# Changing which transfers go first, and where one norm sum stands, in an eight-core decoder layer kernel

## The chip, the cores and the metric

The kernel runs on all 8 cores of one Trainium2 chip, one program per core, each core with its own share of the tokens. The metric is the device time of one launch in microseconds, which is that of the slowest core. Executions fall into a fast state and, now and then, a slow one in which the cores of one die, sometimes of both, run at a lower granted clock. Only fast runs are compared here, and the medians below leave slow runs out.

## The reference, cut to what matters

One decoder layer over 2080 tokens per core (2048 prompt tokens, 16 learned ones before them, 16 tokens of running sequences). Two mixers share one input projection, then comes a gated feed-forward part with a three-tap convolution over tokens. Each half has a norm before and a norm after it.

```python
def rmsnorm(x, g):
    xf = x.astype(jnp.float32)
    y = xf * lax.rsqrt(jnp.mean(xf * xf, axis=-1, keepdims=True) + EPS)
    return (y * g.astype(jnp.float32)).astype(x.dtype)
...
    h = rmsnorm(x, g_pre_mix)
    z = h @ w_in                                                      # (B,T,IN_TOTAL)
    u, v, bg, cg, ga, gb = jnp.split(z, IN_SPLITS, axis=-1)
    ...
    merged = jax.nn.sigmoid(ga) * a + jax.nn.sigmoid(gb) * b
    x = x + rmsnorm(merged @ w_o, g_post_mix)
    h = rmsnorm(x, g_pre_ffn)
    upc, new_ffn = causal_dwconv(h @ w_up, buf_ffn, w_ffn_conv)       # (B,T,2*D_FF)
    gate, val = jnp.split(upc, 2, axis=-1)
    y = (jax.nn.silu(gate) * val) @ w_down
    x = x + rmsnorm(y, g_post_ffn)
```

## The kernel before

Every operation is recorded first. A small scheduler, which models each engine in nanoseconds, then fixes the order of the instructions on each engine, before anything is compiled. Numbers in that model therefore do not change durations; they change orders. TensorE's main work keeps its recorded order. Norm sums are "floating" matmuls: they slip in when their input has been ready for `flt` nanoseconds of the model.

```python
                    if li < len(pe_flt) and not pe_flt[li].nd and (fi == len(pe_fix) or pe_flt[li].idx < pe_fix[fi].idx):
                        f = pe_flt[li]
                        sf = max(free[e], ready[f.idx])
                        if c is None or ready[f.idx] + (f.flt if f.pri > s + 8000.0 else 400.0) <= s or sf <= s - 200.0:
                            c, s = f, sf
# ... cut ...
    def rstd(sq, i, n, lo=0, flt=2500.0, sq2=None):
        tree(sq, n)                          # VectorE: 8 planes of squares to 2, two instructions
        sums([(sq, 0, 2)], n, lo, flt=flt)   # TensorE: sum over partitions, floating
        ln_exp(i, n, lo=lo, sq=sq2)          # ScalarE: reciprocal root
# ... cut ...
    def epi_n2(t):
        rstd(XSQ2[t], 0 if t == NTA - 1 else 2, TA[t], lo_of(t, LO), flt=2500.0 if t == NTA - 1 else 4000.0)
```

The front: x of tile 0 (512 tokens) comes in four quarters through SyncE's DMA queue. The weight blocks of `w_in` (524 KB each, cast to bf16 on the way) and then x of tile 1 (392 tokens, `X[1]`) come through GpSimd's queue. The first `M0` groups of tile 0 are multiplied before tile 1 begins. The first five work on x that is only scaled, and the norm is applied afterwards.

```python
    xs0 = [sp_dma(X[0].flat[:, 0:2 * N0], xT[0][:, 0:2 * N0], [], [X[0].t(0, 2)], 128 * 2 * N0 * 4,
                  pri=-1e6)]
# ... cut: constants, quarters 1 to 3 ...
    wd = [wload(W_IN, w_in, 0, 1, BL)]
    wd += [wload(W_IN, w_in, i, 1, BL, after=[xs0[0]]) for i in range(1, 16)]
# ... cut: other weights ...
    for q in range(4):
        pool_dma(X[1].flat[:, 2 * q * NA:2 * (q + 1) * NA], xT[1][:, 2 * q * NA:2 * (q + 1) * NA], [], [X[1].t(2 * q, 2)],
                 128 * 2 * NA * 4, after=[xs0[1]], pri=-1e6)

    warm(60)
# ... cut: squares and scaling of x0 ...
    for q in range(4):
        pe([(bank(SB, N0), ONES, XSQ2[0].ap[:, k, :]) for k in (2 * q, 2 * q + 1)], [ONESB.t(), XSQ2[0].t(2 * q, 2)],
           [("ps", SB)], N0, start=q == 0, stop=q == 3)
        if q < 3:
            warm(10)
    ln_exp(0, N0, sq=1)
# ... cut ...
    seq = [(0, i) for i in range(NRAW, M0)] + [(1, i) for i in range(NRAW)] + [(0, i) for i in range(M0, M1)]
```

`warm(n)` issues n dummy matmuls so that TensorE's clock is not halved while it waits.

Of the kernel before, what the change touches and what calls it, by code (L numbers as in the profile page):

```python
# [44 lines left out]
FSEQ = (("v", 0), ("c", 0), ("v", 1), ("c", 1), ("u", 0), ("b", 0), ("v", 2), ("c", 2),  # L45
        ("b", 1), ("v", 3), ("c", 3), ("b", 2), ("u", 1), ("b", 3), ("u", 2), ("u", 3))
NRAW = 5
M0, M1 = 6, 12
WIN_ORDER = [{"u": 0, "v": 4, "b": 8, "c": 12}[_k] + _c for _k, _c in FSEQ]
for _c in range(8):  # L50
    WIN_ORDER += [16 + _c, 24 + _c]
# [11 lines left out]
class Sched:  # L63
# [55 lines left out]
    def order(self):  # L119


        ops = self.ops
        for op in ops:
            op.succ = []
            op.nd = len(op.deps)
        for op in ops:
            for d in op.deps:
                ops[d].succ.append(op)
        at, t = {}, 0.0
        for op in ops:  # L130
            if op.eng == "pe" and not op.flt:
                at[op.idx] = t
                t += op.dur
        for op in reversed(ops):
            op.pri = at.get(op.idx, t + 1e5)
            for x in op.succ:
                op.pri = min(op.pri, x.pri - 100.0)
            if op.idx not in at:
                op.pri -= op.byts / 300.0 + 3000.0 if op.dma else 1.5 * op.dur
        ready = {}  # L140
        avail = {e: [] for e in self.ENGS}
        pe_fix = [op for op in ops if op.eng == "pe" and not op.flt]
        pe_flt = [op for op in ops if op.eng == "pe" and op.flt]
        fi = li = 0
        free = {e: 0.0 for e in self.ENGS}
        dma_free = {"sp": 0.0, "pool": 0.0}
        seqs = {e: [] for e in self.ENGS}
        ends = {"sp": [0.0] * 14, "pool": [0.0] * 16}
        tab = None
        cold = 0.0  # L150
        for op in ops:
            ready[op.idx] = 0.0
            if op.nd == 0:
                avail[op.eng].append(op)
        left = len(ops)
        while left:
            best = None
            for e in self.ENGS:
                a = avail[e]
                if e == "pe":  # L160
                    c = s = None
                    if fi < len(pe_fix) and not pe_fix[fi].nd:
                        c = pe_fix[fi]
                        s = max(free[e], ready[c.idx])
                    if li < len(pe_flt) and not pe_flt[li].nd and (fi == len(pe_fix) or pe_flt[li].idx < pe_fix[fi].idx):
                        f = pe_flt[li]
                        sf = max(free[e], ready[f.idx])
                        if c is None or ready[f.idx] + (f.flt if f.pri > s + 8000.0 else 400.0) <= s or sf <= s - 200.0:
                            c, s = f, sf
                    if c is None:  # L170
                        continue
                else:
                    if not a:
                        continue
                    s = max(free[e], min(ready[x.idx] for x in a))
                    c = min((x for x in a if ready[x.idx] <= s), key=lambda x: x.pri + x.off + (SWITCH if x.tab not in (None, tab) else 0.0) - (DMAEARLY if x.dma and e == "pool" else 0.0))
                    if c.tab not in (None, tab):
                        near = [x for x in a if x.tab == tab and ready[x.idx] <= s + 400.0]
                        if near:
                            c = min(near, key=lambda x: x.pri + x.off)  # L180
                            s = max(s, ready[c.idx])
                if best is None or s < best[0]:
                    best = (s, e, c)
            s, e, op = best
            avail[e].remove(op)
            if e == "pe":
                if op.flt:
                    li += 1
                else:
                    fi += 1  # L190
            left -= 1
            seqs[e].append(op)
            op.start = s
            if op.dma:
                s = max(s, ends[e].pop(0))
                free[e] = s + (650.0 if e == "pool" else 400.0)
                b, n = max(free[e], dma_free[e]), op.byts / 300.0
                if e == "sp" and dma_free["pool"] > b:
                    dma_free["pool"] += n
                    n *= 2.0  # L200
                dma_free[e] = b + n
                op.end = dma_free[e] + (3200.0 if e == "pool" else 2400.0)
                ends[e].append(op.end)
            elif e == "pe":
                if s - free[e] > 3400.0:
                    cold = s + 3500.0
                d = op.dur * (2.0 if s < cold else 1.0)
                free[e] = s + d
                op.end = free[e] + 165.0
            else:  # L210
                if op.tab not in (None, tab):
                    tab = op.tab
                    s += 1300.0
                op.end = s + op.dur
                free[e] = op.end + (30.0 if e == "pool" else -85.0)
            for x in op.succ:
                if x.eng == "pe":
                    lat = 0.0 if e == "pe" else 145.0
                elif op.dma:
                    lat = 600.0  # L220
                else:
                    lat = 180.0 if x.eng == "pool" else 100.0
                ready[x.idx] = max(ready[x.idx], op.end + lat)
                x.nd -= 1
                if x.nd == 0:
                    avail[x.eng].append(x)
        self.seqs = seqs
        self.model_end = max(op.end for op in ops)
# [51 lines left out]
def build_nc():  # L280
# [105 lines left out]
    H2S = [XSQ2[0]] + per_tile(KC, True, [o_h2s] * NTA)[1:4] + [XSQ2[4]]  # L386
    MERGED = per_tile(KC, True, [o_merged] * NTA)
    RAW = [MERGED[0], Buf(o_gt, KC, NA, True)]
    PS = [(0, 1), (2, 1)] + [(0, None)] * 3
    H = per_tile(KC, True, [o_h1 if t % 2 else o_h0 for t in range(NTA)])  # L390
    GT = per_tile(4, False, [o_gt] * NTA)
    POOLED = per_tile(4, True, [POOLB.off, o_h2s] + [POOLB.off] * 3)
# [61 lines left out]
    def act(fn, r, w, n, psum=False, ap=0, **k):  # L454
        S.add("act", fn, r, w, dur=n / 1.2 + (170 if psum else 200) + 93 * ap, **k)
# [65 lines left out]
    def ln_exp(i, n, sq=None, lo=0, ps_out=False):  # L521
        s = SD.ap[:, i, lo:n]
        out, tok = (bank(SB, n, lo), ("ps", SB)) if ps_out else (s, SD.t(i, 1))
        act(lambda e: e.activation(out=s, in_=bank(SB, n, lo), func=AF.Ln, bias=cc(C_EPS)),
            [("ps", SB), "eps"], [SD.t(i, 1)], n, psum=True, ap=1, tab="ln")
        if sq is not None:
            s2 = SD.ap[:, sq, lo:n]
            act(lambda e: e.activation(out=s2, in_=s, func=AF.Exp, scale=-1.0), [SD.t(i, 1)], [SD.t(sq, 1)], n, tab="ln")
        act(lambda e: e.activation(out=out, in_=s, func=AF.Exp, scale=-0.5), [SD.t(i, 1)], [tok], n, tab="ln")  # L529

    def rstd(sq, i, n, lo=0, flt=2500.0, sq2=None):
        tree(sq, n)
        sums([(sq, 0, 2)], n, lo, flt=flt)
        ln_exp(i, n, lo=lo, sq=sq2)
# [7 lines left out]
    def prenorm(t):  # L542
        for q in range(4):
            prenorm_sq(t, q)
        rstd(H[t], PS[t][0], TA[t], sq2=PS[t][1] if t == 1 else None)
        for k in range(KC):
            prenorm_h(t, k)

# [6 lines left out]
    def lo_of(t, lo):  # L555
        return lo if t == 0 else 0
# [190 lines left out]
                hook()  # L747

    def epi_n1(t):
        rstd(XSQ2[t], 0 if t == NTA - 1 else 1, TA[t], lo_of(t, LO), flt=5000.0 if t == NTA - 1 else 2500.0)  # L750

    def epi_r(t, q):
        N, lo = TA[t], lo_of(t, LO)
# [18 lines left out]
                   [R[t].t(4 * h, 4)], [("y", t, h)], 128 * 4 * N * 4)  # L772

    def epi_n2(t):
        rstd(XSQ2[t], 0 if t == NTA - 1 else 2, TA[t], lo_of(t, LO), flt=2500.0 if t == NTA - 1 else 4000.0)

    def epi_x(t, k):
        N, lo = TA[t], lo_of(t, LO)
# [119 lines left out]
    def warm(n):  # L898
        pe([(bank(6, 128), ONES, ONES)] * n, [ONESB.t()], [("ps", 6)], 128)
# [10 lines left out]
    S.add("pool", lambda e: e.memset(U.ap[:, :, 0:16], 0.0), [], [U.t()], dur=150)  # L910
    S.add("dve", lambda e: e.memset(cc(C_EPS), EPS), [KCST], ["eps"], dur=100)
    wd = [wload(W_IN, w_in, 0, 1, BL)]
    wd += [wload(W_IN, w_in, i, 1, BL, after=[xs0[0]]) for i in range(1, 16)]
    wload(W_POOL, w_pool, 0, 8, 128, after=[xs0[1]])
    for m in range(8):
        wd += [wload(W_IN, w_in, 16 + 2 * m + i, 1, BL, after=[xs0[1]]) for i in range(2)]
# [1 line left out]

    for q in range(4):
        pool_dma(X[1].flat[:, 2 * q * NA:2 * (q + 1) * NA], xT[1][:, 2 * q * NA:2 * (q + 1) * NA], [], [X[1].t(2 * q, 2)],  # L920
                 128 * 2 * NA * 4, after=[xs0[1]], pri=-1e6)

    warm(60)
    for q in range(4):
# [4 lines left out]
    for q in range(4):  # L929
        pe([(bank(SB, N0), ONES, XSQ2[0].ap[:, k, :]) for k in (2 * q, 2 * q + 1)], [ONESB.t(), XSQ2[0].t(2 * q, 2)],  # L930
           [("ps", SB)], N0, start=q == 0, stop=q == 3)
        if q < 3:
            warm(10)
    ln_exp(0, N0, sq=1)
    for i in range(NRAW):
        F_block(0, i)
# [65 lines left out]
    load_h2(0)  # L1002

    WD = {5: 0, 7: 1, 10: 2, 12: 3, 14: 4, 16: 5, 19: 6, 21: 7}
    WD1 = {7: 0, 9: 1, 11: 2, 13: 3, 15: 4, 17: 5, 19: 6, 21: 7}
    dn = [0]

    def wdn():
# [171 lines left out]
```

## Time and profile before

Median 826.31 us of 3 runs (824.86 to 827.02). All eight cores do nearly the same, so the table gives medians over the cores of the profiled run, with the range where it matters. "Half-clock loss" is half of the time in which TensorE was busy at a granted clock of 0.5.

| Profile before | us |
|---|---|
| x0's quarters land | 5.8, 9.9, 13.4, 16.1 |
| last part of X1 lands | 28.1 (27.5 to 29.1) |
| tile 1's first matmul, after 6 groups of tile 0 | 30.5 (29.2 to 31.1) |
| TensorE idle from 20 to 60 us; half-clock loss there | 0.80; 0.28 |
| TensorE idle from 340 to 440 us; half-clock loss there | 3.58; 1.67 |
| end of the core | 824.3 (818.5 to 825.8) |

TensorE is the full engine, so only its idle or half-clock time can be won, and it lies in two places: the front, and one gap near 400 us where TensorE stands still for a norm sum. The prediction below shows the lines.

To read them: PE, PEld, DVE, ACT, POOL and SP are TensorE, its weight loads, VectorE, ScalarE, GpSimd and SyncE. A timeline row gives start and duration in us, engine, line of the kernel, operation, what is written and read, shapes, count, and in brackets the idle time before it with what ended that. L469 is the helper through which all matmuls go, so its rows are told apart by their column counts (512 or 500 for tile 0, 392 for tile 1). A "tap" is one of VectorE's multiply-adds of the three-tap convolution; it reads a PSUM bank (TensorE's output buffer), which TensorE can write again only afterwards.

### The profile page before, as it was taken

Reading aid. Unit: us, or ns where it says so; the run is one execution under the profiler, and the core shown is the slowest. Engines: PE = TensorE matmul, PEld = TensorE weight load, DVE = VectorE, ACT = ScalarE, POOL = GpSimd, SP = SyncE. Lnnn points to the kernel's source line nnn. Section 1 sums busy time; section 2 is a strip of 40 time slices with the busy share of each in tenths; the row PEclk is TensorE's granted clock in tenths of the full one; section 3 lists DMA queues with packets and bytes.
Section 4 is the critical chain, followed back from the end, with each engine's and each line's share of the span. In section 5 each row is a group of like instructions: output and inputs, shape, how many; then the busy total and the mean of one; then the engine's idle time right before and its main releaser. Section 6 shows DMA issues by size and latency. Waiting matters only on the chain.

```text
span 825.8 us, 16706 instructions; the slowest of 8 cores (818.5 to 825.8 us)
## 1 busy us (share of the span) xinstructions
PE 801.0 (97%) x5108; PEld 499.0 (60%) x5108; DVE 564.7 (68%) x1054; ACT 452.1 (55%) x902; POOL 261.9 (32%) x297
## 2 busy tenths in 40 slices
PE   6999999999999999999899999999999999999994
PEld 4455455555555555566566666666666666666662
DVE  2997448786976686488985676568566765785723
ACT  3523284665565545586754565457456554665532
POOL 6432002001201262399532243225222522252231
PEclk8999999999999999999999999999999999999997
DMA  9999705766027899999970033014101500050063
GB/s 182 198 152 158 149 4 122 179 161 155 25 55 157 128 125 201 189 156 164 190 121 0 2 69 61 1 36 67 39 1 36 70 2 1 2 69 2 1 134 74
DMA packets 62838, 75.16 MB, mean 91 GB/s; under 512 B 3072, under 2 KB 59264, under 8 KB 62736
## 3 DMA queue, kind: packets, MB, share of 16 engines
q0 software_dynamic: 41440, 44.97, 38.2%
q1 hardware_dynamic: 21312, 29.14, 12.6%
q8 instruction: 43, 0.70, 0.3%
q14 instruction: 43, 0.35, 0.1%
HBM read 81.53 MB, written 22.90 MB: 126 GB/s over the span
## 4 chain that ended last, share of the span: by engine, by line
PE 92%; DMA 4%; DVE 2%; issue 1%; ACT 1%; DVEq 0%; SPq 0%; ACTq 0%; POOLq 0%
PE ps L469 92%; DMA big<-w_up 2%; DMA big<-xT 2%; DVE big L551 0%; DVEq L1051 0%; DVE big L820 0%; DVE big L864 0%; SPq L476 0%; DVE big L718 0%; ACT big L539 0%; ACT big L816 0%; DVE big L945 0%; ACT big L847 0%; DVE big L782 0%; DVE big L716 0%
## 5 line engine op out<-in xcount | busy, mean ns | idle before, releaser
L469 PE MATMUL ps<-big 128*128 128x346 bf16 (+4 forms) x5108 | 801.0, 320 | 13.5 <-ACT big L539 4.6
L469 PEld LDWEIGHTS ps<-big 128*128 128x128 bf16 x5108 | 499.0, 99 | 315.3 <-issue 21.5
L820 DVE SCALAR_TENSOR_TENSOR big<-ps,big 128x344 f32<-128x344 f32 (+1 forms) x528 | 281.6, 570 | 95.5 <-ACT big L816 72.6
L834 POOL TENSOR_TENSOR big<-big 128x344 bf16<-128x344 f32 x132 | 125.1, 950 | 262.5 <-DVE big L820 186.4
L816 ACT ACTIVATE big<-ps,big 128x344 f32<-128x344 f32 (+1 forms) x264 | 139.7, 542 | 71.2 <-PE ps L469 64.9
L833 ACT ACTIVATE big<-big 128x344 f32<-128x344 f32 x132 | 64.6, 490 | 42.3 <-DVE big L820 40.5
L699 ACT ACTIVATE big<-ps 128x392 f32<-128x392 f32 (+1 forms) x80 | 39.7, 514 | 62.7 <-PE ps L469 38.7
L480 POOL DMA_DIRECT2D big<-xT x16 | 15.7, 1004 | 155.3 <-DVE big L712 148.0
L844 ACT ACTIVATE big<-ps,big 128x344 f32<-128x344 f32 x48 | 26.0, 546 | 57.6 <-PE ps L469 57.4
L482 POOL DMA_DIRECT2D big<-w_up x44 | 33.5, 768 | 56.8 <-PE ps L469 49.7
L712 DVE SCALAR_TENSOR_TENSOR big<-ps,big 128x392 f32<-128x392 f32 (+1 forms) x40 | 25.8, 646 | 36.1 <-PE ps L469 34.6
L513 DVE TENSOR_TENSOR big<-big 128x1568 bf16<-128x1568 bf16 (+3 forms) x28 | 24.4, 873 | 33.4 <-ACT big L731 30.0
L480 POOL DMA_DIRECT2D yT<-big x21 | 27.4, 1539 | 31.4 <-DVE big L864 17.1
L850 DVE TENSOR_TENSOR big<-big 128x688 bf16<-128x688 bf16 x17 | 8.8, 517 | 41.7 <-ACT big L847 41.7
L729 ACT ACTIVATE big<-ps,big 128x392 f32<-128x392 f32 (+1 forms) x40 | 24.6, 614 | 16.8 <-PE ps L469 10.2
L608 DVE TENSOR_TENSOR big<-big 128x406 f32<-128x406 f32 (+7 forms) x50 | 30.1, 602 | 1.5 <-DVE big L614 0.2
L847 ACT ACTIVATE big<-ps 128x344 bf16<-128x344 f32 x48 | 21.6, 450 | 13.3 <-PE ps L469 13.3
L482 POOL DMA_DIRECT2D big<-w_in x32 | 23.1, 742 | 17.8 <-DMA big<-w_in 10.4
L580 DVE SCALAR_TENSOR_TENSOR big<-big 128x392 f32<-128x392 f32 (+1 forms) x40 | 25.5, 646 | 3.4 <-ACT big L577 2.8
L718 DVE TENSOR_TENSOR big<-big 128x392 bf16<-128x392 f32 (+1 forms) x40 | 24.3, 617 | 2.3
L577 ACT ACTIVATE big<-big 128x392 f32<-128x392 f32 (+1 forms) x20 | 12.7, 637 | 23.4 <-DVE big L663 23.1
L782 DVE SCALAR_TENSOR_TENSOR big<-big 128x392 bf16<-128x392 f32 (+1 forms) x40 | 24.5, 659 | 0.4 <-ACT big L529 0.4
(59 smaller groups left out, 350.4 us busy)
## 6 DMA issues: line engine op xcount, KB each, us to landing
big<-w_up POOLq DMA_DIRECT2D x44, 256.0 KB, 10.6
big<-w_in POOLq DMA_DIRECT2D x32, 256.0 KB, 24.1
yT<-big POOLq DMA_DIRECT2D x21, 344.0 KB, 5.8
big<-xT POOLq DMA_DIRECT2D x16, 392.0 KB, 8.0
yT<-big SPq DMA_DIRECT2D x8, 784.0 KB, 7.9
big<-w_dn POOLq DMA_DIRECT2D x8, 704.0 KB, 15.9
big<-xT SPq DMA_DIRECT2D x6, 784.0 KB, 5.9
big<-h2T SPq DMA_DIRECT2D x6, 692.0 KB, 5.1
```

Source lines behind the costliest of these rows:

```text
L469: ins = e.matmul(o, lhsT=l, rhs=x, start=(start and i == 0), stop=(stop and i == last))
L480: return S.add("pool", lambda e: e.dma_start(out=out, in_=in_, accum_op=ALU.add, max_dma_last_dim=mx), r, w, dma=True, byts=byts, pri=pri, ...
L482: return S.add("pool", lambda e: e.dma_start(out=out, in_=in_, max_dma_last_dim=mx), r, w, dma=True, byts=byts, pri=pri, after=after)
L580: dve(lambda e, k=k: e.scalar_tensor_tensor(out=cv, in0=p[:, 2 + k + lo:2 + k + N], scalar=cc(C_WC + 4 * k + c), in1=cv, op0=ALU.mult, op1 ...
L608: dve(lambda e, nx=nx, cur=cur, s=s, a2=a2: e.tensor_tensor(out=nx[:, a2:W], in0=cur[:, a2:W], in1=cur[:, a2 - s:W - s], op=ALU.add), [ct] ...
L699: act(lambda e, b=b, g=g: e.activation(out=GT[t].ap[:, g, lo:N], in_=bank(b, N, lo), func=AF.Sigmoid), [("ps", b)], [GT[t].t(g, 1)], N, ps ...
L712: dve(lambda e: e.scalar_tensor_tensor(out=A_, in0=bank(bp, N, lo), scalar=cc(C_PS + m), in1=A_, op0=ALU.mult, op1=ALU.mult), [("ps", bp), ...
L816: act(lambda e, b=b, fj=fj, tt=tt: e.activation(out=tt[:, 0:n], in_=bank(b, n), func=AF.Copy, scale=cc(C_WF + fj)), [("ps", b), KCST], [to ...
L820: dve(lambda e, b=b, fj=fj, tt=tt, k=k: e.scalar_tensor_tensor(out=tt[:, 0:n], in0=ps[:, b * 512 + k:b * 512 + k + n], scalar=cc(C_WF + 44 ...
L833: act(lambda e: e.activation(out=g, in_=g, func=AF.Silu), [T.t(0, 1)], [T.t(0, 1)], NB, tab="silu")
L834: S.add("pool", lambda e: e.tensor_tensor(out=gb.ap[:, j, :], in0=g, in1=v, op=ALU.mult), [T.t()], [gb.t(j, 1)], dur=NB * 2.17 + 100)
L844: act(lambda e: e.activation(out=Y.ap[:, m, :], in_=bank(b, NB), func=AF.Copy, scale=cc(C_G4 + m)), [("ps", b), KCST], [Y.t(m, 1)], NB, ps ...
```

## The change

The intent: x0 shall have the DMA engines to itself but for the first weight block (later blocks wait for x0's second quarter instead of its first); eight groups of tile 0 instead of six shall cover the time until X1 is there; more dummies keep the clock up; and the sum of the last tile's second norm shall stand late enough that TensorE does not wait for it. Some numbers of the scheduler's model change with it.

```diff
-M0, M1 = 6, 12
+M0, M1 = 8, 12
@@ scheduler
-        dma_free = {"sp": 0.0, "pool": 0.0}
+        dma_free = {"sp": 0.0, "pool": 5500.0}
-                        if c is None or ready[f.idx] + (f.flt if f.pri > s + 8000.0 else 400.0) <= s or sf <= s - 200.0:
+                        if c is None or ready[f.idx] + (f.flt if f.pri > s + 8000.0 or f.flt > 5000.0 else 400.0) <= s or sf <= s - 200.0:
-                b, n = max(free[e], dma_free[e]), op.byts / 300.0
-                if e == "sp" and dma_free["pool"] > b:
+                b, n = max(free[e], dma_free[e]), op.byts / (350.0 if e == "pool" else 300.0)
+                if e == "sp" and s > 4000.0 and dma_free["pool"] > b:
@@ ... cut: order of the two exponentials and their rows in ln_exp, rstd, PS ...
@@ epi_n2
-        rstd(XSQ2[t], 0 if t == NTA - 1 else 2, TA[t], lo_of(t, LO), flt=2500.0 if t == NTA - 1 else 4000.0)
+        rstd(XSQ2[t], 0 if t == NTA - 1 else 2, None, TA[t], lo_of(t, LO), flt=5500.0 if t == NTA - 1 else 4000.0)
@@ front
-    wd += [wload(W_IN, w_in, i, 1, BL, after=[xs0[0]]) for i in range(1, 16)]
+    wd += [wload(W_IN, w_in, i, 1, BL, after=[xs0[1]]) for i in range(1, 16)]
-                 128 * 2 * NA * 4, after=[xs0[1]], pri=-1e6)
+                 128 * 2 * NA * 4, after=[xs0[1]])
-            warm(10)
+            warm(20)
-    WD1 = {7: 0, 9: 1, 11: 2, 13: 3, 15: 4, 17: 5, 19: 6, 21: 7}
+    WD1 = {9: 0, 11: 1, 13: 2, 15: 3, 17: 4, 19: 5, 20: 6, 21: 7}
```

## The prediction

> **What bounds the kernel now.** I read the page first: is one engine full, and where is it not?
>
> ```profile
> PE 801.0 (97%) x5108; PEld 499.0 (60%) x5108; DVE 564.7 (68%) x1054; ACT 452.1 (55%) x902; POOL 261.9 (32%) x297
> PE   6999999999999999999899999999999999999994
> PEclk8999999999999999999999999999999999999997
> ```
>
> TensorE is busy for 97% of the span; only the first slices, slice 20 and the last are short. The change moves no matrix work but 30 dummy matmuls, so all it can win is idle or half-clocked TensorE time. Second, who TensorE waits for:
>
> ```profile
> PE ps L469 <- ACT big L539: 4.6, 3, 2.8
> PE ps L469 <- DVE big L513: 3.6, 1, 3.6
> PE ps L469 <- POOL big L910: 2.9, 1, 2.9
> PE ps L469 <- ACT big L847: 0.9, 2, 0.6
> PE ps L469 <- ACT big L942: 0.8, 1, 0.8
> ```
>
> L539 squares x as its quarters land, L942 scales the second tile's x, L513 adds squares up for a norm, L910 is set-up. Third, TensorE's timeline at the start (tile 0 is 512 tokens, tile 1 is 392) and near 400 us:
>
> ```profile
> 12.49 1.15 PE L469 MATMUL ps<-big 128*128 128x512 bf16 x12 [2.77 <-ACT big L539]
> 15.13 2.08 PE L469 MATMUL ps<-big 128*128 128x512 bf16 x12 [1.49 <-ACT big L539]
> 17.59 12.67 PE L469 MATMUL ps<-big 128*128 128x512 bf16 x50 [0.37 <-ACT big L539]
> 31.05 29.18 PE L469 MATMUL ps<-big 128*128 128x392 bf16 x153 [0.80 <-ACT big L942]
> ...
> 400.54 11.76 PE L469 MATMUL ps<-big 128*128 128x392 bf16 x68 [3.57 <-DVE big L513]
> ```
>
> Useful work starts at 17.59 us with the last two norm matmuls; then come six groups of tile 0 (8 matmuls each); tile 1 starts at 31.05. After that nothing stops TensorE until 397. Fourth, why x0 is late, from the chain of waits and from one stretch before, one during the mixing of queues and one at half clock (last three columns: granted clock, DMA share, GB/s):
>
> ```profile
> 2.90 13.40 DMA big<-xT
> 16.39 1.06 ACT big L539
> ...
> 4.00:5.00 1.00, 1.00 (x12) 1.00 (x11) 0.00 (x0) 0.00 (x0) 0.00 (x0) 1.00 0.91 296
> 7.00:8.00 1.00, 1.00 (x13) 1.00 (x12) 0.00 (x0) 0.90 (x1) 1.00 (x2) 1.00 1.10 209
> ...
> 18.00:20.00 2.00, 2.00 (x6) 0.71 (x5) 0.00 (x0) 1.16 (x2) 2.00 (x4) 0.50 1.11 160
> ```
>
> x0 alone gets about 290 GB/s. By the packets of the trace, from about 5 us on its queue drops to some 150 GB/s, while the weight queue writes 50 GB/s of bf16 (100 read as f32). The quarters land at 5.5, 11.2, 13.9 and 16.3.
>
> **What the Trainium skill says.** "DMA: Bandwidth & Descriptors", section "Queues, rings and completion order": each DMA engine takes its queues in turn, packet by packet. The trace agrees: one weight block in the other queue is enough to halve x0's rate. "HBM Reference", section "Specifications (TRN2)": about 358 GB/s for a core whose neighbour streams as well. Agrees: w_in blocks (524 KB read) land 1.5 us apart once x0 is in, 345 GB/s. "TensorE: Matmul & The Clock Gate", Part 1: an idle window of some 3.4 us halves the clock. Agrees: from the end of the gap before 400.54 the clock records show 3.4 us at 0.5, and 6.8 us from 14.7 on; but the section's account leaves open which gap cools it, and of the eight cores two, with gaps of 1.4 and 3.5 us near 397, stayed warm.
>
> **The change part by part.**
>
> *x0.* Up to the second quarter's landing (median 9.9 us over the cores) nothing changes: the completions show that only block 0, which stays early, was then competing; blocks 1 to 5 queued behind it. So x0 does not finish at 10 us, as 2.2 MB at 290 GB/s would give. At 10 us about 0.65 MB of x0 are still to come. Block 0 ends near 11.3, blocks 1 onward are issued 0.6 us after the quarter and flow 1 to 2 us later: x0 has some 0.2 MB at the mixed rate and the rest nearly alone, plus 0.5 us for the last completion, so 13.2 instead of 16.2. Squares 1.06 and the norm matmuls put the first group at 14.95, at full clock because 20 dummy matmuls (1.1 us) fill each gap instead of 10. Before, 3.9 us of work ran at half clock.
>
> *M0 from 6 to 8.* The queue before tile 1's x holds two more blocks, 1.05 MB or 3 us. X1's last part landed at 28.2 (median). From 13.2, 5.1 MB remain until it lands; at the 290 GB/s of this phase that is 17.6, so 30.8, plus 0.6 for the scaling: tile 1 starts at 31.2 to 31.5 (median before 30.5). The new instruction order puts the scalings of X1 behind no wait on a convolution, as the 0.80 gap had it. Eight groups of 1.69 take 13.5, so TensorE is through at 28.5 and then waits 2.7 us for X1. The win is two groups, 3.37, minus 0.75 for the later start: 2.6 us. That wait may cool the clock: half of 3.4 us lost at 30%, minus 0.5. Front: 2.1 us. Most of x0's 3 us is thus hidden behind X1; what is kept is work done ahead.
>
> *Order of the two exponentials.* The reciprocal root is now computed first and its square second. Same count; H of tile 0 is ready 0.7 us sooner after x0, off the path.
>
> *The last tile's second norm.* Its sum may now wait up to 5.5 us; in the order it stands 40 matmuls later, 40 x 0.147 = 5.9 us. VectorE's order is unchanged there:
>
> ```profile
> 395.77 1.61 DVE L513 TENSOR_TENSOR big<-big 128x1568 bf16<-128x1568 bf16 x1
> 397.31 2.50 DVE L820 SCALAR_TENSOR_TENSOR big<-ps,big 128x344 f32<-128x344 f32 x5
> 399.73 0.66 DVE L513 TENSOR_TENSOR big<-big 128x784 bf16<-128x784 bf16 x1
> 400.31 3.71 DVE L820 SCALAR_TENSOR_TENSOR big<-ps,big 128x344 f32<-128x344 f32 x7
> ```
>
> The tree ends at 400.4 and TensorE would come at 402.9: the 3.57 goes, and with it 1.7 (half of the 3.4 us at half clock). But the gap also let VectorE catch up. At 397 TensorE has written the first half of a pair of groups while VectorE still works on the pair three before it, and a group can only start when the group seven before it has left its bank, since seven banks rotate. Each pair costs VectorE four taps (L820), 0.53 us each in the rows above, and TensorE two groups of 1.17 us. Walking on from 397.0: the first group finds its bank free; the second, at 398.2, needs a tap that is the third of the five in the 397.31 row and ends at 398.85, so it waits 0.8; the fifth, at 402.5, waits 0.15; the rest run until the four to five L782 (0.55 each) of the new norm stand in VectorE's order, then one group waits 0.85, near 412. From there w_down groups (22 matmuls with no taps) give VectorE room. So 1.8 comes back as small waits, too short to cool the clock. Net 5.3 - 1.8 = 3.5; I take 3.7, as waits of under a microsecond are at the edge of what these rows resolve.
>
> *Other sums.* The DMA model of the scheduler is now faster, so the sums of the second norms of tiles 1 to 3 stand 2 to 4 groups earlier. Setting where the tree can end against where TensorE now asks for it: tile 1, tree 208.0 (its two steps now adjoin), TensorE 211.5; tile 3, both move together, 1.7 us of slack stays; tile 2, tree 268.5 (first step at 267.07 plus 0.97 and 0.56), TensorE 267.7. So one wait of up to 0.8, by half likely: minus 0.4. The later w_down groups in the second FFN tile meet no wait now and cost nothing.
>
> Sum: 2.1 + 3.7 - 0.4 = 5.4; 826.3 - 5.4 = 820.9 us.
>
> **Rivals.** (1) x0 is truly alone and X1 follows at 330 GB/s, landing at 29.4; the front gives 4 and the mid-kernel gap its full 5.3: 817. For it: blocks and X1 landed at 325 GB/s between 16.9 and 28. Against it: block 0's interleaving. (2) X1 lands at 32, its wait grows to 4 us and cools TensorE: the front gives nothing, total 822 to 823. For it: engines that finish x0 early idle until blocks 1 onward flow. (3) VectorE becomes the bound from 397 to 420, it is over 95% busy there from 406: the gap is only spread, 824. Against it: it sits idle 0.4 to 0.7 us at a time when TensorE feeds it slower. (4) The last sums come too early and stall: 1 to 3 us back.
>
> **Range and chances.** One core in eight that is unlucky sets the time (818.5 to 825.8 before), which widens it: 817.0 to 824.3. 2% is 16.5 us; all idle and cold time outside the set-up and the tail is about 15 us, so faster is 1%, slower 1%.
>
> **What would show it.** Right: x0's last quarter lands near 13; no half clock before 25; a TensorE wait for L944 (the scaling of X1) of 2 to 3.5 us just before the 392-column groups at 31; the 3.6 us L513 wait gone, small waits for L822 taps near 398 to 413. Wrong: x0 in by 11, X1 in by 29, a half-clock stretch after 31, or a lasting wait for the L513 of an earlier tile.

## The result, and the profile after

The changed kernel took 824.83 us (median; 824.09 to 826.24, 4 runs) against 826.66 us (824.86 to 827.06, 4 runs) of the kernel before on the same chip. The ratio is 0.9984, with a 95% interval of 0.9964 to 1.0004. Ratios here are the mean time of one kernel's fast runs over that of the other's fast runs of the same rounds, so not quite the ratio of the medians. That is 1.3 to 1.8 us won instead of the 5.4 predicted, and half a microsecond above the predicted range; the interval includes 1, so by itself even this gain is not clear of noise. In the profiled run the medians over the cores are:

| | before | after |
|---|---|---|
| x0's last quarter lands | 16.1 | 13.8 (13.4 to 14.9) |
| last part of X1 lands | 28.1 (27.5 to 29.1) | 31.8 (30.9 to 34.4) |
| tile 1's first matmul | 30.5, 6 groups done | 33.1 (32.1 to 35.6), 8 groups done |
| idle 20 to 60 us; half-clock loss | 0.80; 0.28 | 3.15; 1.43 |
| idle 340 to 440 us; half-clock loss | 3.58; 1.67 | 0.24; 0 |
| end of the core | 824.3 (818.5 to 825.8) | 819.9 (816.9 to 822.5) |

The median core gained 4.4 us. The slowest core of the profiled run, which sets the time, gained 3.3. Both figures flatter the change: the profiled run after (824.09) was the fastest of its four, and the one before (827.37) was slower than the four timed beside the change. The busy and clock rows of the slowest core after (core 1), from the page:

```profile
PE 799.4 (97%) x5138; PEld 499.5 (61%) x5138; DVE 565.1 (69%) x1054; ACT 452.1 (55%) x902; POOL 262.8 (32%) x297
PE   6799999999999999999999999999999999999994
PEclk9899999999999999999999999999999999999998
```

Slice 20 is full now. The waits of TensorE on the same core (in all, times, longest):

```profile
PE ps L469 <- DVE big L947: 4.4, 1, 4.4
PE ps L469 <- ACT big L541: 2.7, 3, 1.7
PE ps L469 <- DMA big<-w_in: 1.1, 2, 0.7
PE ps L469 <- DVE big L822: 0.2, 1, 0.2
```

The 3.6 us wait for the adds of squares (L513 before) is gone and the waits for x0's squares (L541, L539 before) fell from 4.6 to 2.7. In their place stands one wait of 4.4 us for L947, the scaling of X1, and two for weight blocks. On TensorE's timeline of this core:

```profile
14.08 3.83 PE L469 MATMUL ps<-big 128*128 128x512 bf16 x32 [0.48 <-ACT big L541]
18.29 1.85 PE L469 MATMUL ps<-big 128*128 128x500 bf16 x8 [0.38 <-DMA big<-w_in]
20.85 10.42 PE L469 MATMUL ps<-big 128*128 128x500 bf16 x48 [0.71 <-DMA big<-w_in]
35.63 10.73 PE L469 MATMUL ps<-big 128*128 128x392 bf16 x48 [4.36 <-DVE big L947]
```

Useful work starts earlier than before, is through with eight groups at 31.3, and then stands still until 35.63. The chain that ended last says why (start, duration, what):

```profile
1.95 8.65 DMA big<-xT
...
11.18 6.16 POOL big L482 x9
...
17.90 16.53 DMA big<-xT
...
34.95 0.43 DVE big L947
...
35.63 375.34 PE ps L469 x2220
```

x0's second quarter landed at 10.61; only then did GpSimd issue the weight blocks (L482), and X1, which stands behind them, landed at 34.44. From 35.63 to 413.30 TensorE is not stopped at all. The stretches of this core (the last three columns are granted clock, DMA share, GB/s) show the price at both ends:

```profile
12.00:13.00 1.00, 1.00 (x15) 0.77 (x14) 0.11 (x1) 0.12 (x1) 1.00 (x2) 1.00 0.63 228
13.00:14.00 1.00, 0.60 (x11) 0.42 (x8) 1.00 (x3) 0.99 (x2) 1.00 (x2) 1.00 0.20 41
...
38.00:40.00 2.00, 2.00 (x8) 0.90 (x7) 2.00 (x5) 0.36 (x1) 1.25 (x2) 0.50 1.19 168
```

Between 13 and 14 us the DMA engines were 20% busy, in a phase in which everything waits for transfers. This hole is core 1's own: on the other seven cores they were 83% busy or more in that microsecond. After the gap before tile 1 the granted clock is 0.5, which costs this core another 2.4 us. Five of the eight cores were cooled like this. Near 400 us, core 2 shows what can remain there:

```profile
395.66 13.53 PE L469 MATMUL ps<-big 128*128 128x346 bf16 x90 [0.81 <-DVE big L822]
410.44 19.78 PE L469 MATMUL ps<-big 128*128 128x346 bf16 x134 [1.25 <-DVE big L822]
```

These are two short waits for the taps of VectorE (L822, L820 before), 2.1 us together. Core 3 has them as 0.2 and 1.3 us. On the other six cores only the later one is there, with 0.2 us.

The theory after this look: the late sum gives all that is won, and the front costs. x0's earlier arrival only lengthens the wait for X1, which then cools the clock. Rivals: the front gives a little and the late sum less than thought; or `M0` = 8 is what costs; or the gate on the second quarter is innocent and the dummies or model numbers are to blame.

### The profile page after: what moved, and what is told of

Read it like the earlier page. It is cut to its first block, busy times and chain, and to the rows that moved or that the text cites. A ratio compares the mean times of both kernels' runs of the same rounds, so it can differ in the third digit from the quotient of the medians.

```text
span 822.5 us, 16751 instructions; the slowest of 8 cores (816.9 to 822.5 us)
## 1 busy us (share of the span) xinstructions
PE 799.4 (97%) x5138; PEld 499.5 (61%) x5138; DVE 565.1 (69%) x1054; ACT 452.1 (55%) x902; POOL 262.8 (32%) x297
## 4 chain that ended last, share of the span: by engine, by line
PE 94%; DMA 3%; POOL 1%; DVE 1%; issue 0%; DVEq 0%; ACT 0%; SPq 0%; ACTq 0%; POOLq 0%
PE ps L469 94%; DMA big<-xT 3%; POOL big L482 1%; DVEq L1053 0%; DVE big L866 0%; DVE big L784 0%; ACT big L849 0%; SPq L476 0%; DVE big L822 0%; ACT big L524 0%; ACT ps L527 0%; DVE big L947 0%; DVE big L873 0%; DVEq L272 0%; ACTq L272 0%
## 5 line engine op out<-in xcount | busy, mean ns | idle before, releaser
L469 PE MATMUL ps<-big 128*128 128x346 bf16 (+6 forms) x5138 | 799.4, 319 | 12.1 <-DVE big L947 4.4
L822 DVE SCALAR_TENSOR_TENSOR big<-ps,big 128x344 f32<-128x344 f32 (+1 forms) x528 | 281.4, 569 | 95.3 <-ACT big L818 74.6
L482 POOL DMA_DIRECT2D big<-w_up x44 | 33.5, 768 | 58.1 <-PE ps L469 48.6
L714 DVE SCALAR_TENSOR_TENSOR big<-ps,big 128x392 f32<-128x392 f32 (+1 forms) x40 | 25.8, 645 | 35.2 <-PE ps L469 32.1
L513 DVE TENSOR_TENSOR big<-big 128x1568 bf16<-128x1568 bf16 (+3 forms) x28 | 24.4, 873 | 29.1 <-ACT big L733 28.5
L731 ACT ACTIVATE big<-ps,big 128x392 f32<-128x392 f32 (+1 forms) x40 | 24.5, 612 | 14.2 <-PE ps L469 13.6
L482 POOL DMA_DIRECT2D big<-w_in x32 | 23.1, 741 | 23.7 <-DMA big<-w_in 12.2
L579 ACT ACTIVATE big<-big 128x392 f32<-128x392 f32 (+1 forms) x20 | 12.8, 638 | 30.2 <-DVE big L665 30.1
L849 ACT ACTIVATE big<-ps 128x344 bf16<-128x344 f32 x48 | 21.6, 450 | 11.3 <-PE ps L469 11.3
```

Source lines behind the costliest of these rows:

```text
L469: ins = e.matmul(o, lhsT=l, rhs=x, start=(start and i == 0), stop=(stop and i == last))
L482: return S.add("pool", lambda e: e.dma_start(out=out, in_=in_, max_dma_last_dim=mx), r, w, dma=True, byts=byts, pri=pri, after=after)
L714: dve(lambda e: e.scalar_tensor_tensor(out=A_, in0=bank(bp, N, lo), scalar=cc(C_PS + m), in1=A_, op0=ALU.mult, op1=ALU.mult), [("ps", bp), ...
L822: dve(lambda e, b=b, fj=fj, tt=tt, k=k: e.scalar_tensor_tensor(out=tt[:, 0:n], in0=ps[:, b * 512 + k:b * 512 + k + n], scalar=cc(C_WF + 44 ...
```

## The experiments

All results were correct. Runs 1 to 4 shared one chip and its runs of the kernel before (median of the fast ones 827.05), runs 5 to 8 another (827.32), runs 9 and 10 a third (827.35). Each had five rounds. "Measured" gives the median of the fast runs and their ratio to the kernel before with its 95% interval.

Two limits hold throughout. The changed kernel was not timed again beside these runs, so it is compared through ratios, and a difference of 0.25% between two ratios is about as large as its own uncertainty. And one profile is one sample: in four kernels with the same transfers at the start (the changed one and runs 2, 5 and 8), the last part of X1 landed at 31.8, 32.8, 32.6 and 32.7 in the median; the profile of the changed kernel is the earliest of them.

### 1. The late sum alone

The kernel before, with only this edit:

```diff
-... (f.flt if f.pri > s + 8000.0 else 400.0) <= s ...
+... (f.flt if f.pri > s + 8000.0 or f.flt > 5000.0 else 400.0) <= s ...
-  flt=2500.0 if t == NTA - 1 else 4000.0)
+  flt=5500.0 if t == NTA - 1 else 4000.0)
```

> The kernel before with only the sum of the last tile's second norm moved 40 matmuls later; start of the kernel untouched. My theory: this one part holds the whole gain of the change. The 3.6 us wait near 397 and the half clock after it go and at most 0.3 us comes back, so a median core gains about 5 us and the time falls by 4 to 5 us, to about 822. The prediction's own step (1.8 us comes back as waits for PSUM banks): 3.5 us, 823. Rival, VectorE is the bound there and the gap is only spread: 0 to 1 us.

Measured: 823.36 us; 0.9960 (0.9944 to 0.9975). TensorE's timeline of its slowest core:

```profile
400.01 13.54 PE L469 MATMUL ps<-big 128*128 128x346 bf16 x90 [0.88 <-DVE big L820]
414.81 10.40 PE L469 MATMUL ps<-big 128*128 128x346 bf16 x70 [1.26 <-DVE big L820]
```

The gap of 3.6 us and its half clock are gone on every core, and tap waits of 0.2 to 2.4 us in all took their place (on this core another 1.4 us for ScalarE as well). Median idle from 340 to 440 us fell from 3.58 to 1.69 and the half-clock loss from 1.67 to 0: 3.6 us recovered, and the time fell by 0.40% of 827.05, or 3.3 us. By the ratios this one edit wins more than the whole change, though the two intervals overlap; run 2 is the direct test.

### 2. The rest of the change alone

The changed kernel, with the last tile's second sum put back to where it stood before:

```diff
-  flt=5500.0 if t == NTA - 1 else 4000.0)
+  flt=400.0 if t == NTA - 1 else 4000.0)
```

> The changed kernel with the late sum put back to the place it had before (312 matmuls in), all else of the change kept. My theory: the front part loses. The 3.6 us wait near 397 is back, tile 1 starts at 33 to 35 us, TensorE idles 2 to 5 us for X1 and most cores cool; median core 0 to 1 us slower than before, the slowest core 2 to 4 us slower, 828.5 to 830. The prediction's step: front gains 2.1 us, 824.5. Rival, the front is neutral: 826 to 827.

Measured: 829.65 us; 1.0026 (1.0011 to 1.0042). The rest of the change makes the kernel slower, and the interval is clear of 1. On TensorE's timeline of its slowest core both waits are there, the new one and the old one:

```profile
33.60 14.58 PE L469 MATMUL ps<-big 128*128 128x392 bf16 x65 [3.76 <-ACT big L944]
...
403.18 22.11 PE L469 MATMUL ps<-big 128*128 128x392 bf16 x138 [3.61 <-DVE big L513]
```

(L944 is the scaling of the odd rows of X1 on ScalarE, and L513 the adding of squares.) Medians: idle 3.66 from 20 to 60 us, half-clock loss 2.16. The parts add up: -0.40% and +0.26% make -0.14%, and the whole change measured -0.16%.

### 3. Six groups instead of eight

```diff
-M0, M1 = 8, 12
+M0, M1 = 6, 12
```

> The changed kernel with six groups of tile 0 ahead of tile 1 instead of eight. My theory: one weight block costs the DMA queue 1.6 to 1.8 us and gives TensorE 1.69 us of work, so M0 moves nothing: tile 1 starts 3.4 us earlier with two groups fewer done, the same wait of 2 to 5 us for X1, time within 0.7 us of the changed kernel (824 to 825.5). The prediction's step (two groups of work ahead are worth up to 2.6 us): 826 to 827.5.

Measured: 825.39 us; 0.9985 (0.9966 to 1.0004), the same as the changed kernel. Tile 1 starts at 30.1 with six groups done, 3.0 us earlier than in the changed kernel with eight. Idle (3.27) and half-clock loss (1.52) are the same too. Two more groups are 3.4 us of work, but two more blocks ahead of X1 take as long: in the changed kernel the blocks land 1.72 us apart on core 4 (15.82 to 26.16 for six), and a group takes 1.69. So `M0` is neutral and not what costs.

### 4. The gate back on the first quarter

```diff
-    wd += [wload(W_IN, w_in, i, 1, BL, after=[xs0[1]]) for i in range(1, 16)]
+    wd += [wload(W_IN, w_in, i, 1, BL, after=[xs0[0]]) for i in range(1, 16)]
```

> The changed kernel with blocks 1 to 15 waiting for x0's first quarter again, as before; instruction order on every engine the same. My theory: waiting for the second quarter leaves the DMA engines partly idle between 12 and 15 us on some cores and delays X1, which is what tile 1 waits for; without it X1's last part lands at 31.3 or a little earlier on all cores (now 30.9 to 34.4), x0 lands at 16 again, the wait for X1 shrinks below 1.5 us, no half clock after 30, so the slowest core gains 2 to 4 us: 821 to 823. Rival, x0 first is what helps: tile 1 no earlier, TensorE cold from 14 to 21 us, time equal or 1 to 2 us worse than the changed kernel.

Measured: 823.40 us; 0.9958 (0.9945 to 0.9972). The orders of TensorE, GpSimd and SyncE stay as they were; a few instructions of VectorE and ScalarE swapped neighbours. x0's last quarter lands at 16.0 again, 2.2 us later. X1's last part lands at 31.75, as in the changed kernel, but its spread is 30.5 to 32.2 instead of 30.9 to 34.4. Tile 1 starts at 32.7. Idle from 20 to 60 us is 1.10 instead of 3.15, and no core is cooled after 30 us. The slowest core's line at that point:

```profile
33.30 15.02 PE L469 MATMUL ps<-big 128*128 128x392 bf16 x81 [1.88 <-DVE big L677]
```

(L677 is VectorE's work on tile 0; it ended 0.1 us after the last scaling of X1, at 33.27.) So with x0 later, the median core starts tile 1 no later. The time that x0 had saved was only waited away, and the gate on the second quarter is what turned the front into a loss: on the same chip this kernel is clear of run 2, and of run 3, which equals the changed kernel, by 0.27%. It keeps the twenty dummies, the order of the exponentials and the new model numbers, so these together are not what costs. The mid-kernel waits are back to 2.0 us here, so part of what the front returns goes there. One thing was not steady: run 9 has the same front, and in its profile three cores were cooled after the wait for X1. The early gate makes that rarer, not impossible.

### 5. Dummies in the wait for X1

Forty dummy matmuls (2.4 us) in the spare bank, put right before tile 1's first group after the order is fixed; nothing else moves:

```diff
+        at = s.seqs["pe"].index(s.ops[first1[0]])       # tile 1's first group
+        # op issues 40 x e.matmul(bank(SB, 128), lhsT=ONES, rhs=ONES, start=True, stop=True)
+        s.seqs["pe"].insert(at, op)
```

> The changed kernel with 40 dummy matmuls (2.2 us) on TensorE just before tile 1's first group, where it waits for X1; all other instructions in the same order. My theory: part of the front's loss is the half clock after that wait (five of eight cores of the changed kernel, 1.4 to 2.7 us); filled, the wait cools no core, so the slow cores gain 1.4 to 2.7 us and the time falls to 822.5 to 823.8. Rival, the clock after the wait does not matter to the slowest core, or the fill only delays tile 1: 825 to 826.

Measured: 823.53 us; 0.9958 (0.9941 to 0.9975). TensorE's timeline of the slowest core (L1066 are the dummies):

```profile
30.23 2.40 PE L1066 MATMUL ps<-big 128*128 128x128 bf16 x40
33.61 14.69 PE L469 MATMUL ps<-big 128*128 128x392 bf16 x79 [0.99 <-DVE big L948]
```

The wait is as long as before, but it is filled: no core is at half clock after it, against 1.43 us lost on the median core and 2.4 to 2.7 on the two slowest. If all of the difference between 0.9984 and 0.9958 is due to this, it is worth 2.1 us, with an uncertainty as large. So cooling looks like the larger part of what the front costs on the slowest core; that it is removed is shown, its share of the launch time is an estimate. The mid-kernel waits are back here too (2.10 us in the median).

### 6. The gate on the third quarter

```diff
+        for op in win[1:16]:                 # weight blocks 1 to 15, after the order is fixed
+            op.deps.discard(xs0[1].idx)
+            op.deps.add(xs0[2].idx)
```

> The changed kernel with blocks 1 to 15 waiting for x0's third quarter instead of its second; same order on every engine. My theory: a dose more of what hurts. x0 lands at most 0.7 us earlier, block 1 lands 2 to 3 us later, X1 lands 1.5 to 3 us later (33.5 to 35), time 826.5 to 828. Rival, giving x0 the engines longer pays: 823.5 to 825.

Measured: 828.88 us; 1.0017 (1.0004 to 1.0030). Block 1 lands at 18.5 and X1 at 35.55, 3.7 us later than in the changed kernel. x0 is no earlier for it (14.2). TensorE now waits for the blocks too; the slowest core's timeline:

```profile
22.41 3.57 PE L469 MATMUL ps<-big 128*128 128x500 bf16 x16 [1.40 <-DMA big<-w_in]
...
36.41 11.75 PE L469 MATMUL ps<-big 128*128 128x392 bf16 x56 [4.52 <-ACT big L944]
```

The dose works: a later gate delays X1 and gives x0 nothing. The interval is clear of 1, so this kernel is slower than the one before.

### 7. The first block waits as well

```diff
+        win[0].deps.add(xs0[1].idx)          # block 0 behind the second quarter, issued just ahead of block 1
```

> The changed kernel with block 0 waiting for x0's second quarter too, so that x0 has the engines truly to itself until then; same order otherwise. If block 0 is what slows x0: the second quarter lands near 7.2, the last near 10.5 (now 13.8), blocks flow from 10 to 11 without a gap in between, X1's last part lands at 29 to 30, tile 1 starts at 30 to 31, the wait for X1 stays near 3 us, time 821.5 to 823.5. Rival, the queues' packet turns do not matter and total traffic alone sets X1: x0 earlier by under 1 us, X1 at 32, time 824 to 826.

Measured: 827.64 us; 1.0003 (0.9988 to 1.0018). x0 is now really alone until its second quarter, yet that quarter lands at 9.17 in the median, against 9.47 in the changed kernel. The stretches of core 0:

```profile
4.00:5.00 1.00, 1.00 (x13) 1.00 (x11) 0.00 (x0) 0.00 (x0) 0.00 (x0) 1.00 1.03 328
...
6.00:7.00 1.00, 0.59 (x11) 0.42 (x8) 0.63 (x3) 0.99 (x2) 0.00 (x0) 1.00 0.98 238
```

With only x0 under way, its rate still falls from 328 to 238 GB/s while the engines show as busy. The prediction laid the slow second quarter to block 0, which shares the engines packet by packet; that was only part of it. By the packets of the traces, x0's queue moved 158 GB/s from 5 to 9 us beside block 0 (changed kernel, median of the cores) and 234 alone (this run), against about 296 from 4 to 5 us. So block 0 does slow x0, and the last quarter lands 1.9 us earlier without it, at 11.92; what slows x0 when it is alone stays open. It buys nothing: block 0 lands at 15.4 (up to 18.9), X1 at 33.3, and idle and half-clock loss from 20 to 60 us grow to 3.79 and 2.03.

### 8. Ten dummies between the norm matmuls, as before

```diff
-            warm(20)
+            warm(10)
```

> The changed kernel with 10 dummy matmuls between the norm matmuls again instead of 20; same order. My theory: tile 0's groups may run at half clock for some us around 15 to 20, but the wait for X1 shrinks by as much, so the time stays within 0.8 us of the changed kernel (824 to 825.6). Rival, the warm clock is worth its 2 us: 826 to 827.

Measured: 825.41 us; 0.9981 (0.9965 to 0.9998), the same as the changed kernel. The granted clock is at half for 3.4 to 6.8 us before 20 us on all eight cores, against one core of the changed kernel. So the twenty dummies do keep the clock up. That what TensorE does faster there is waited away before X1 fits the unchanged time, but the profiles alone do not show it: TensorE comes to the wait about 1 us later here, and in this run X1 happened to land 0.9 us later too, so the wait is hardly shorter (2.94 against 3.15).

### 9. Where the tap waits near 400 us come from

The prediction took them for VectorE having too little room. The traces say something else. ScalarE's evacuation of the last tile's mixer output (L731) writes into the buffer from which the y store of tile 3 still reads. Core 4 and core 2 of the changed kernel, ScalarE's timeline (one line each):

```profile
335.91 0.59 ACT L731 ACTIVATE big<-ps,big 128x392 f32<-128x392 f32 x1 [1.50 <-DMA yT<-big]
```

```profile
338.98 0.59 ACT L731 ACTIVATE big<-ps,big 128x392 f32<-128x392 f32 x1 [4.02 <-DMA yT<-big]
```

Core 2, where the store landed later, has both tap waits, and core 4 has only the 0.2. On SyncE the load of the first feed-forward block (`h2T`) stands ahead of the second half of that store. Run 9 is run 4 with these two swapped:

```diff
+        y = s.ops[s.last_w[("y", 3, 1)]]     # second half of tile 3's y store
+        q.remove(y)
+        q.insert(q.index(s.ops[ld0]), y)     # ld0: load of the first h2 block
```

> This is the kernel whose weight blocks wait for x0's first quarter only (run before: 0.9958, 2.0 us of TensorE idle between 340 and 440 us), with one swap in SyncE's order after scheduling: the second half of tile 3's y store is issued ahead of the load of the first h2 block, and nothing else moves. Theory: the two VectorE-tap waits (0.8 and 1.25 us) come from that store, which lands so late that ScalarE's evacuation into its source buffer waits 1.5 to 4 us, and the adds, the tree and the taps behind it with it. Then the store lands some 3 us earlier, ScalarE waits under 1 us for it, the mid idle falls from 2.0 to 0.5 us or less on the median core, and the ratio to the kernel before is 0.993 to 0.995. Rival (VectorE simply has too little room there, as the prediction had it): mid idle stays 1.8 to 2.3 us, ratio 0.995 to 0.997. Risk: the h2 load lands later and TensorE waits for it at the start of the first FFN tile.

Measured: 826.56 us; 0.9985 (0.9963 to 1.0007), on another chip than run 4. The mechanism is confirmed and the time is not. TensorE's timeline of core 2, where one short tap wait is left:

```profile
408.42 16.85 PE L469 MATMUL ps<-big 128*128 128x346 bf16 x114 [0.30 <-DVE big L822]
```

All eight cores are like this: one tap wait of 0.2 to 0.3 us, whereas seven of eight had 0.7 to 2.1 us in run 4. But the load that had to step back is late now on five of the eight cores. On the slowest, core 4:

```profile
344.00 18.30 PE L469 MATMUL ps<-big 128*128 128x346 bf16 x112 [2.41 <-DMA big<-h2T]
```

This gap cooled the clock too and cost another 1.7 us. Not all of the lost time is the swap's, though: cores 3, 4 and 5 were also cooled after waits of 2.2 to 2.5 us for X1, at 1.65 to 1.71 us each, which the same front did to no core in run 4. The DMA engines are full in this stretch (in the changed kernel's core 2 the 40-slice DMA row from 300 to 345 us is at 9 nearly throughout), so one transfer's gain may well be another's loss; no run isolates that.

### 10. The early gate, the dummies and the swap together

Runs 4, 5 and 9 in one kernel.

> The best version I can name: the changed kernel with weight blocks after x0's first quarter, 40 dummy matmuls right before tile 1's first group, and the y store ahead of the h2 load. Front theory: with the early gate the wait for X1 is 1 us and does not cool, so the dummies add at most nothing and cost up to 1 us where X1 lands early: idle 20 to 60 us 0.3 to 1.5, no half clock; ratio the same as the run beside it within 0.1%, 0.993 to 0.995. If the dummies are worth something with the early gate too, it is 0.1 to 0.2% faster than the run beside it.

Measured: 825.11 us; 0.9971 (0.9952 to 0.9990), on the same chip as run 9. The front is clean: median idle 0.05 us from 20 to 60 us, no half clock there. The load of the first feed-forward block costs up to 3.8 us and cools two cores. It is not faster than runs 1, 4 and 5. Those beat the kernel before clearly, and the changed kernel by about the uncertainty (0.9960, 0.9958 and 0.9958 against 0.9984); of these run 1 is the smallest edit.

## Why the prediction was right or wrong

**That the change is worth well under 2% was right, its size was not.** 820.9 us was predicted and 824.83 came; of the sum of gains, 5.4 us, the largest term held and the front's had the wrong sign.

**The front (predicted +2.1, measured about -2).** This is the step that failed: "the win is two groups, 3.37, minus 0.75 for the later start", less 0.5 for a clock that "may cool". The rest of the change alone (run 2) measured +0.26% in time, that is 2.2 us lost, and the changed kernel against the late sum alone (0.9984 and 0.9960) says 2.0. In the profiled run tile 1 started 2.6 us later in the median and not 0.75 (33.1 against 30.5), so the two groups won 0.7 and not 2.6; the half-clock loss from 20 to 60 us grew by 1.15 on the median core and by more on the slowest. So the median core lost about 0.4 us and the slowest, which sets the time, some 2. By its terms:
- x0: predicted at 13.2, landed at 13.8; block 0, to end "near 11.3", landed at 13.2. That block 0 was what slowed x0 was half of the cause (run 7), which was harmless in size. No half clock before 25 was right for seven of eight cores. (x0 is 2.1 MB, four quarters of 524 KB, and not 2.2; nothing hangs on it.)
- X1: predicted at 30.8, landed at 31.8, and at 33.4 and 34.4 on the two slowest cores. The prediction used one rate for all cores: its 17.6 us from x0's landing to X1's were 18.0 in the median but 20.6 and 19.9 on these two. It also put tile 1 "0.6 for the scaling" after the landing; it took 1.2 on all eight cores (1.18 to 1.36). So two more groups are not gained but paid for (run 3).
- The wait for X1: predicted 2.7, measured 3.15 in the median and 4.4 on the slowest core.
- Cooling: predicted "at 30%, minus 0.5"; it came on five of eight cores and took 2.4 to 2.7 us from the two slowest. Run 5 puts it at about 2.1 us of the launch, give or take as much. Since the slowest of eight cores sets the time, a 30% chance on one core is close to a certainty for one of eight (94% if the cores are independent); to multiply the loss by 30% was the basic mistake. "A half-clock stretch after 31" was the prediction's own sign of being wrong, and it came.
- Rival (2) of the prediction, "X1 lands at 32, its wait grows to 4 us and cools TensorE", is what happened (X1 at 31.8, a wait of 4.4 us on the slowest core); it was only given too little weight, and it stopped at "the front gives nothing" where it cost.

**The last tile's second norm (predicted +3.7, measured 3.3).** Right in size by run 1, and the waits of 0.8 and 0.85 us near 398 and 412 appeared as 0.8 and 1.25 on the cores that have them. The reason given for them was incomplete: they come when the y store of tile 3 lands late and everything behind ScalarE's evacuation slips (run 9), not from VectorE's load alone. So the right size is in part luck. Why the changed kernel's own profile shows them on two cores only stays open: that its slow front brings the others there later, when the store has landed, does not fit core 4, the earliest of all, which has none either.

**The other sums (predicted -0.4).** No stall appeared in the changed kernel: TensorE was idle for 0.00 us between 60 and 340 us on each of its cores. In other kernels some cores lose up to 2.2 us between 60 and 340 us; those waits were not followed up.

**Left open:** what slows x0's second quarter when it is alone, and why on two cores of the changed kernel the blocks after the gate landed some 2 us later than on the others (block 1 at 18.2 and 18.8, the rest at 15.6 to 17.5).

## What to carry to other kernels

An input that arrives earlier is worth only what the next input lets through: before giving one transfer the engines, find which transfer the engine will wait for next, and whether the gate delays that one. A wait of 2 to 4 us on TensorE should be costed with the half clock that can follow it, and on eight cores a chance of cooling per core must be counted as near-certain for the slowest; dummies inside such a wait kept the clock up on all eight cores (run 5). When a change has two separable parts, measure each alone: here an edit of two lines in the scheduler carried the whole gain and the larger rest ate more than half of it. And profile a kernel more than once before explaining a difference of a microsecond.

## What the Trainium skill lacked or had wrong

- "TensorE: Matmul & The Clock Gate", Part 1, gives as the condition for the half clock at least one idle window of about 3.4 us. Over the 12 kernels profiled here (96 cores), gaps of TensorE between 20 and 430 us were followed by half clock in 0 of 77 cases from 1 to 2 us, 8 of 14 from 2 to 3 us, 35 of 43 from 3 to 4 us and 6 of 6 above 4 us; the shortest that cooled was 2.21 us, and one of 3.8 us did not. Gaps well below the stated window can cool the clock, and a table of chances by length would have mended the prediction.
- "DMA: Bandwidth & Descriptors", section "Queues, rings and completion order": the packet-by-packet sharing of queues accounts for only a part of x0's slow second quarter. With its queue alone in use, one core moved 328 GB/s from 4 to 5 us and 238 from 6 to 7 us (run 7). "HBM Reference", section "Specifications (TRN2)", gives about 358 GB/s per core; neither explains the dip.
- No page says how long GpSimd's queue takes to come back to its full rate after such a gate, beside another queue; "DMA: Bandwidth & Descriptors" is where it belongs, and it gives only a first-byte latency. In run 7, block 0's first packet came 1.6 to 2.4 us after its issue on the eight cores. On core 1 of the changed kernel, block 1 was issued from 11.18 us on, and from 13 to 14 us the engines were 20% busy and moved 41 GB/s.
